# Two attention stages of a hybrid decoder: from a scheduled order to a fixed stream with two-bank steps

## The chip, the core and the metric

One core of a Trainium2 chip runs the whole program. The metric is the device time in microseconds (us). Engines: PE (matrix multiply, its weight loads listed as PEld), DVE (vector), ACT (scalar), POOL (general), SP (issues DMAs). PE writes its results into PSUM, eight banks of 128 partitions x 512 f32 columns; the other operands are in SBUF.

## What is computed

Two layers over 2048 tokens of width 1024. Layer 0 mixes tokens with multi-head latent attention (12 heads, query and key of 64 + 32 rotary), layer 1 with forgetting attention (12 heads of 64, the cumulated log forget gate added to the logits). Both have 4 heads of cross-attention to 256 memory tokens.

```python
def causal_block_attention(q, k, v, scale, log_f_cum=None):
    s = jnp.einsum('bqhd,bkhd->bhqk', q_i, k) * scale          # for each block of 128 queries
    if log_f_cum is not None:
        s = s + (f_q[..., None] - f_t[:, :, None, :])
    s = jnp.where(key_pos[None, :] <= q_pos[:, None], s, -jnp.inf)
    return jnp.einsum('bhqk,bkhd->bqhd', softmax(s), v)

h = h + rms_norm((concat(main, mem_out) * silu(gate)) @ w_out[i], norm_post[i])
```

## The kernel before

The stages follow each other: `proj_a` and `up_a` (projections of layer 0), the attention of layer 0, `out_proj(0)`, `proj_b` (layer 1), the attention of layer 1, `out_proj(1)`. To keep f32 accuracy each operand is split into a high and a low part (`hi` at L170, `lo` at L189), and a product is two or three matmul passes.

An attention stage works unit by unit. A unit (`Unit`, L1374) is one head and one group g of 512 queries; for a memory head it has 256 keys, for a causal head 512(g+1). A head has 17,408 logit columns of 128 keys each. For each unit there are these parts:

- **Maxima** (`max_closures`, L1421): a matmul at L1454 with queries on the partitions writes up to 512 keys into one bank, and DVE takes the row maximum: a plain reduce at L1461, or at L1458, for the chunk with the diagonal, a custom instruction that adds the causal mask `mqk` first and writes a junk tile, followed by a read of its accumulator. `nm` (L1466) negates, `nm_row` (L1477) transposes through PE (L1480), ACT copies the row (L1482) and issues the small DMA that puts it into the query operand (L1483). That the maximum is then part of the logits matmul is why the row must be there before the unit's logits start.
- **Steps** (`main_closures`, L1487). A wide step has 1024 logit columns, a narrow one 256. A head has 16 wide and 4 narrow steps, a memory unit one wide step. Keys are on the partitions. `s_half` (L1533) works in halves of one bank: matmuls at L1550 (three passes in layer 0, two in layer 1; L1525 and L1529 add the causal mask), ACT's exp of the half from PSUM (L1553), and after the last half ACT's copy to f16 (through L173), and the subtraction that gives the low part (L195), of which POOL does a share and DVE the rest (`POOL_SHARE`, L53: 0.45 of the columns in layer 0, 0.75 in layer 1).
- **Values** (`pv_steps`, L1562): 3 matmuls of 64 or 65 columns (L1575) for each 128x128 block of probabilities, in batches of two steps. `finish` (L1579) divides and stores; ACT issues that DMA (L1592).

`run_units` (L1202) writes the units in program order with maxima ahead of the steps by a count of microseconds (`LEAD`), loads of queries, keys and values in between, and values at a raised priority (L1277). The tile framework then schedules: it takes instructions of all engines by priority when its own model finds them ready, so the order on each engine isn't the written one. Banks: maxima 1 to 4, logits 5 to 7 one at a time, values 0. There are 4 buffers for each of `ph` and `pl` (the f16 high and low parts).

Buffers that a DMA will overwrite are first touched by POOL (`hold`, L1008, a copy of one word), so that the wait for their last reader is POOL's. SP issues nearly all loads (L970 and others), POOL those at L1341. In layer 0 POOL also splits the output weights (`w_split`, L1100: 1024 columns at L180 and L195 for each of 8 tiles). 8 memory units of layer 0 and 12 of layer 1 run early, beside the end of the projections (`att_start`, L973). `out_proj`'s matmuls are at L1173.

Of the kernel before, what the change touches and what calls it, by code (L numbers as in the profile page):

```python
# [21 lines left out]
P = 128  # L22
# [6 lines left out]
G = 512  # L29
# [23 lines left out]
POOL_SHARE = {"mla": 0.45, "fox": 0.75, "mem": 0.5}  # L53
LOGP = 8.0 * math.log(2.0)
# [84 lines left out]


# [12 lines left out]
class Banks:  # L153
# [5 lines left out]
    def tile(self, shape, dtype, name=None, tag=None):  # L159
        self.k += 1  # L160
        return view(self.mem, self.banks[(self.k - 1) % len(self.banks)] * G, shape, dtype, name)


class Trunk:
# [64 lines left out]
    def constants(self, ctx):  # L229
# [16 lines left out]
                                pattern=[[1, P]], channel_multiplier=-1)  # L246
        ones = cp.tile([P, P], F32, name="ones")
# [725 lines left out]
    def att_start(self, l):  # L973
# [5 lines left out]
        else:  # L979
# [8 lines left out]
        ap["qq"] = Turn(*(Later(lambda b=b, k=k: b.tile([P, 2, G], F32R, name=f"qq{k}")) for k, b in enumerate(qqs)))  # L988
        ap["ym"] = Turn(*(ymp.tile([P, 4, 2 * DH], F32, name=f"ym{k}") for k in range(4)))
        ap["nr"] = Turn(*(nrp.tile([4, P], F32R, name=f"nr{k}") for k in range(4)))  # L990
        ap["vrm"] = Turn(vrp.tile([P, MEMH * NMEM // P, DH], F32, name="vrm"))
        mqk = self.mqk = sp.tile([P, G], BF16, name="mqk")
        ap["mj"] = Turn(sp.tile([P, G], BF16, name="mj"))
        ap["pm"], ap["ps"], ap["pv"] = self.banks(2, 3), self.banks(5, 6), self.banks(0)
        self.l, self.yt = l, {}
        nc.gpsimd.memset(mqk, 0.0)
        nc.gpsimd.affine_select(out=mqk[:, G - P:G], in_=mqk[:, G - P:G], compare_op=ALU.is_ge, fill=NEG, base=0,
                                pattern=[[-1, P]], channel_multiplier=1)
# [7 lines left out]
        run_units([mem], first)  # L1006

    def hold(self, word):  # L1008

        self.hi("pool", word, self.ap["nr"].tiles[0][0:1, 0:1].bitcast(F32))  # L1010
# [29 lines left out]
    def attention(self):  # L1040
# [5 lines left out]
        ap["pm"], ap["ps"], ap["pv"] = self.banks(1, 2, 3, 4), self.banks(5, 6, 7), self.banks(0)  # L1046
# [53 lines left out]
        def w_split(c):  # L1100
            w = ap["vr"].next().rearrange("p (c t) d -> p c (t d)", c=2)
            self.hold(w[0:1, 0, 0:1])
            nc.sync.dma_start(out=w, in_=self.i["w_out"][l, c * P:(c + 2) * P, :].rearrange("(c p) d -> p c d", p=P))
            for k in range(2):
                tiles(c + k)
                self.hi("pool", W[c + k][0], w[:, k])
                self.lo("pool", W[c + k][1], w[:, k], W[c + k][0])

        def w_load(c):
            tiles(c)  # L1110
            for k in range(2):
                self.hold(W[c][k][0:1, 0:1])
                self.load_r(W[c][k], self.ws[c, k])
        if l == 0:
            extra = [(4 + c, 0.55, lambda c=c: w_split(c)) for c in range(0, KC, 2)]
# [86 lines left out]
def run_units(heads, objs, extra=()):  # L1202

    n = len(objs)
    maxq, late = [], []
    for u, o in enumerate(objs):
        for j, (f, c) in enumerate(o.max_closures()):
            maxq.append((u, f, c))
            if j == 1 and late:
                maxq.append(late.pop())  # L1210
        maxq.append((u, o.nm, 0.0))
        late.append((u, o.nm_row, 0.0))
    maxq.append(late.pop())
    t = acc = lead = 0.0
    need = [0.0] * n
    for u, f, c in maxq:
        need[u] += c
    span = {}
    rate = sum(need) / sum(c for o in objs for _, _, c in o.main_closures())
    for u, o in enumerate(objs):  # L1220
# [3 lines left out]
        t += sum(c for _, _, c in o.main_closures())  # L1224
        span[o.hd.idx] = (span.get(o.hd.idx, (t0, 0))[0], t)
    lead += LEAD[heads[0].l]
    aux = [(-1.0, hd.idx, f) for hd in heads[len(heads) > 1:2] for _, f in hd.prep()]
# [5 lines left out]
    for h, fr, f in extra:  # L1233
        a, b = span[h + 1]
        aux.append((a + fr * (b - a), 99, f))
    aux.sort(key=lambda x: (x[0], x[1]))
    st = dict(k=0, done=0.0, dma=0)
    pend = []
# [18 lines left out]
    def advance(main, target):  # L1257
        while st["k"] < len(maxq):
            u, f, c = maxq[st["k"]]
            if u > main and not (st["done"] <= target and u <= main + AHEAD):  # L1260
# [5 lines left out]
            f()  # L1266
            st["done"] += c
            st["k"] += 1

    def flush():  # L1270
        while pend:
            o = pend[0][0]
            ends = [x[3] for x in pend if x[0] is o][:BATCH]
            m = len(ends)
# [370 lines left out]
```

## Time and profile before

| what | value |
|---|---|
| median of 3 runs | 2985.06 us (2978.82 to 2997.47) |
| the profiled execution's own time | 2981.39 us |
| its span from first to last instruction | 2979.7 us |
| mean granted PE clock | 0.966 |
| PE, DVE, ACT, POOL busy | 95%, 59%, 44%, 37% of the span |

The attention of layer 0 lies at about 638 to 1294 us of the span, that of layer 1 at 2170 to 2800 us. Busy times are unions of the records of one engine; consecutive records of an engine can overlap, so the distance between starts is shorter than a record.

### The profile page before, as it was taken

How to read it: one execution, taken by the hardware profiler on the slowest of the kernel's cores; microseconds unless marked ns; L12 is line 12 of the kernel's file. 1: busy time of each engine (PE TensorE's matmuls, PEld its weight loads, DVE VectorE, ACT ScalarE, POOL GpSimd, SP SyncE). 2: the span in 40 equal slices, each digit the busy share in tenths (PEclk: the TensorE clock that was granted, in tenths of full speed). 3: DMA queues.
4: the chain of work that ended last, by engine and by line, in shares of the span. 5: the costliest groups of instructions: out<-in, count | busy, mean ns of one | idle time of the engine just before them, and what ended most of it. 6: DMA issues, size and time to landing. Idle time of an engine off the chain costs nothing.

```text
span 2979.7 us, 60697 instructions
## 1 busy us (share of the span) xinstructions
PE 2815.9 (95%) x24017; PEld 2389.2 (80%) x24017; DVE 1765.3 (59%) x3710; ACT 1312.8 (44%) x2315; POOL 1095.8 (37%) x1190
## 2 busy tenths in 40 slices
PE   7999999889999999999999999999889799999999
PEld 6789998657888788788889978998567677777887
DVE  6422215568898999754553364101378799999444
ACT  5321123347777777642230010111257687777421
POOL 2110124344556655642000023100135566676521
PEclk9999999879999999999999999999868899999999
DMA  5332447762343323255343139723433334353453
GB/s 188 127 132 90 126 163 259 248 191 74 80 101 85 90 80 87 80 176 203 128 137 103 59 125 311 236 76 109 129 101 93 102 102 115 103 159 118 166 178 117
DMA packets 261685, 398.23 MB, mean 134 GB/s; under 512 B 25196, under 2 KB 141436, under 8 KB 261292
## 3 DMA queue, kind: packets, MB, share of 16 engines
q1 hardware_dynamic: 146032, 237.25, 27.8%
q10 hardware_dynamic: 113832, 155.32, 14.4%
q8 instruction: 189, 3.10, 0.4%
q0 software_dynamic: 1536, 1.77, 0.3%
q14 instruction: 96, 0.79, 0.1%
HBM read 237.83 MB, written 156.17 MB: 132 GB/s over the span
## 4 chain that ended last, share of the span: by engine, by line
PE 73%; DVE 12%; DMA 8%; issue 3%; ACT 1%; POOL 1%; ACTq 0%; SPq 0%; DVEq 0%; POOLq 0%
PE banks L226 34%; PE banks L1550 12%; PE banks L1173 12%; PE banks L1575 8%; PE banks L1454 4%; DVE bA L195 4%; DVE mx L1461 4%; DVE bA L1458 1%; DMA qs<-bA 1%; PE banks L1148 1%; PE banks L306 1%; DMA qrs<-bA 1%; PE banks L1435 1%; ACT bA L173 1%; DMA bA<-qbs 1%
## 5 line engine op out<-in xcount | busy, mean ns | idle before, releaser
L195 POOL TENSOR_TENSOR bA<-bA,bA 128x768 f16<-128x768 f32 (+7 forms) x306 | 435.8, 1432 | 344.2 <-ACT bA L173 277.2
L226 PE MATMUL banks<-bR,bA 128*128 128x256 f32 (+3 forms) x4437 | 552.9, 287 | 0.6 <-DVE bQ L467 0.6
L226 PEld LDWEIGHTS banks<-bR,bA 128*128 128x128 f32 x4437 | 544.3, 190 | 5.4 <-DVE bQ L467 0.8
L226 PE MATMUL banks<-bA,bR 128*128 128x512 f32 (+2 forms) x2208 | 515.0, 389 | 6.7 <-ACT bS L780 4.2
L1553 ACT ACTIVATE bA<-banks 128x512 f32<-128x512 f32 (+1 forms) x771 | 419.9, 569 | 216.4 <-PE banks L1550 124.6
L1550 PE MATMUL banks<-bA,bA 96*128 96x512 f32 (+13 forms) x1808 | 499.8, 381 | 5.0 <-DMA bA<-bA 2.5
L226 PEld LDWEIGHTS banks<-bA,bR 128*128 128x128 f32 x2208 | 401.3, 191 | 93.5 <-ACT bS L780 4.9
L1461 DVE TENSOR_REDUCE mx<-banks 128x1 f32<-128x512 f32 x576 | 377.3, 679 | 39.3 <-PE banks L1454 37.4
L1550 PEld LDWEIGHTS banks<-bA,bA 96*128 96x128 f32 (+3 forms) x1808 | 324.7, 195 | 46.8 <-DMA bA<-bA 3.1
L173 ACT ACTIVATE bA<-bA 128x1024 f16<-128x1024 f32 (+5 forms) x335 | 280.9, 853 | 143.6 <-PE banks L1575 34.0
L1454 PE MATMUL banks<-bA,bA 73*128 73x512 f32 (+5 forms) x864 | 292.0, 398 | 23.4 <-DVE mx L1458 14.0
L195 DVE TENSOR_TENSOR bA<-bA,bA 128x256 f16<-128x256 f32 (+4 forms) x267 | 250.5, 942 | 89.8 <-ACT bA L173 89.6
L195 DVE TENSOR_TENSOR bR<-bR,bR 128x1024 fp32r<-128x1024 f32 (+6 forms) x134 | 136.1, 1018 | 189.2 <-POOL bR L180 169.4
L195 POOL TENSOR_TENSOR bR<-bA,bR 128x512 f16<-128x512 f32 (+2 forms) x167 | 183.7, 1102 | 165.6 <-ACT bR L173 87.6
L1575 PEld LDWEIGHTS <-bA 128*128 128x128 f16 x5280 | 183.8, 101 | 55.1 <-issue 27.3
L1173 PE MATMUL banks<-bA,bA 128*128 128x512 f32 x960 | 227.4, 391 | 0.0
L1454 PEld LDWEIGHTS banks<-bA,bA 73*128 73x128 f32 (+1 forms) x864 | 163.2, 199 | 69.3 <-DVE mx L1458 23.6
L1550 PE MATMUL banks<-bR,bA 128*128 128x512 f32 (+6 forms) x624 | 212.6, 405 | 3.2 <-ACT bA L1553 1.9
L1575 PEld LDWEIGHTS <-bR 128*128 128x128 f16 x5280 | 174.2, 99 | 45.1 <-issue 15.9
L180 POOL TENSOR_SCALAR bR<-bR 128x1024 fp32r<-128x1024 f32 (+3 forms) x50 | 60.5, 1212 | 406.8 <-PE banks L226 367.5
L1173 PEld LDWEIGHTS banks<-bA,bA 128*128 128x128 f32 x960 | 178.5, 188 | 36.1
L1575 PE MATMUL banks<-bA,bR 128*128 128x65 f16 (+1 forms) x4896 | 175.2, 195 | 9.3 <-DVE bR L195 7.9
(218 smaller groups left out, 3607.1 us busy)
## 6 DMA issues: line engine op xcount, KB each, us to landing
bA<-qbs SPq DMA_DIRECT2D x65, 256.0 KB
bA<-in_x_dram SPq DMA_DIRECT2D x32, 512.0 KB
gs<-bG ACTq DMA_DIRECT2D x128, 128.0 KB
bA<-gs SPq DMA_DIRECT2D x32, 512.0 KB
bA<-ys SPq DMA_DIRECT2D x32, 512.0 KB
bA<-h SPq DMA_DIRECT2D x28, 512.0 KB
ks<-bA ACTq DMA_DIRECT2D x24, 512.0 KB
qs<-bA ACTq DMA_DIRECT2D x24, 512.0 KB
```

The source lines that it names most:

```text
L173: nc.scalar.activation(out, in_, AF.Copy, scale=scale)
L180: nc.gpsimd.tensor_scalar(out, in_, scale, 0.0, op0=ALU.mult, op1=ALU.add)
L195: e.tensor_tensor(out=out, in0=in_, in1=hi, op=ALU.subtract)
L226: nc.tensor.matmul(out, lhsT=a, rhs=b, start=start and i == 0, stop=stop and i == n - 1)
L306: nc.tensor.transpose(pt[:, j, :], out[:, c * P:(c + 1) * P], self.idf)
L1148: nc.tensor.transpose(pt[:, j, :], gt[:, c * P:(c + 1) * P], self.idf)
L1173: nc.tensor.matmul(ps[:, ns], lhsT=a, rhs=b[:, ns], start=c == 0 and j == 0, stop=c == KC - 1 and j == 2)
L1454: nc.tensor.matmul(ps[:, 0:w], lhsT=q[0:qr, t * P:(t + 1) * P], rhs=k[0:kr, c * G:c * G + w], start=True, stop=True)
L1461: nc.vector.tensor_reduce(out=self.mx[:, t, c:c + 1], in_=ps[:, 0:w], axis=AX.X, op=ALU.max)
L1550: nc.tensor.matmul(ps[:, o:o + bw], lhsT=k[0:kr, (self.k0 + kt) * P:(self.k0 + kt + 1) * P], rhs=q[0:qr, q0:q0 + bw], start=i == 0 and not ...
L1553: nc.scalar.activation(pf[:, half:half + hw], ps[:, 0:hw], AF.Exp, scale=self.scale)
L1575: nc.tensor.matmul(self.pv[:, t, 0:n], lhsT=p[:, o:o + P], rhs=v[:, kv, a:a + n], start=self.first, stop=False, skip_group_check=True)
```

## The change

Both attentions are emitted inside `manual_schedule` for PE, ACT, DVE, POOL and SP: each engine gets these instructions in the order in which they are written.

- A step is one piece (`flow`): logits of both halves in two neighbouring banks of a ring of four (banks 4 to 7), one exp of up to 1024 columns, one f16 copy, and for wide steps one POOL subtraction of all 1024 columns. DVE subtracts for narrow steps only, one step later (`flow_lo`).
- Maxima have banks 1 to 3. The causal mask is added by a matmul of 128 columns, and the plain reduce writes the negated maximum. The constant that `nm` added is now the bias of the exp. The row's copy is DVE's and its DMA SP's; so is the DMA of the result.
- There are 6 `ph` and 6 `pl` buffers (5 at the end of layer 1); values are written 3 steps behind the logits, half of a step's maxima ahead of its logits and half behind.
- All `hold`s are gone, and the load at L1341 goes to SP. In layer 0 the output weights are loaded before their split, and split in 32 pieces of 256 columns, the high part by ACT.
- Early memory units are written by `run_early`, one unit of maxima ahead, still scheduled by the framework.

```diff
+    def flow(self, blocks, box):
+        K, nc, ap = self.K, self.K.nc, self.K.ap
+        w = box["w"] = max(b[1] + b[3] for b in blocks)
+        ps = ap["ps"].tile([P, 2 * G], F32, name="ps", tag="ps")
+        pf, ph, pl = (ap[x].next() for x in ("pf", "ph", "pl"))
+        box.update(pf=pf, ph=ph, pl=pl)
+        for half in range(0, w, G):
+            self.s_bank(blocks, half, box, ps[:, half:half + G])
+            self.s_logits(blocks, half, box[half])
+        nc.scalar.activation(pf[:, 0:w], ps[:, 0:w], AF.Exp, scale=self.scale, bias=LOGP)
+        K.hi("act", ph[:, 0:w], pf[:, 0:w])
+        if w > G:
+            K.lo("pool", pl[:, 0:w], pf[:, 0:w], ph[:, 0:w])
+    def flow_lo(self, box):
+        w = box["w"]
+        if w <= G:
+            self.K.lo("dve", box["pl"][:, 0:w], box["pf"][:, 0:w], box["ph"][:, 0:w])
...
-        ap["pm"], ap["ps"], ap["pv"] = self.banks(1, 2, 3, 4), self.banks(5, 6, 7), self.banks(0)
+        ap["pm"], ap["ps"], ap["pv"] = self.banks(1, 2, 3), BankRing(self.psum, 4, 4), self.banks(0)
...
-        run_units(heads, units, extra)
+        order = {getattr(mybir.EngineType, x) for x in ("PE", "Activation", "DVE", "Pool", "SP")}
+        with self.tc.manual_schedule(engines=order):
+            run_units(heads, units, extra, fewer)
...
+    for i, (u, s, w) in enumerate(steps):
+        o = objs[u]
+        run_aux(t)
+        lag[0] = len(K.ap["ph"].tiles) - 3
+        todo = advance(u, min(t * rate + lead, RUNUP * (t + 4 * G) + need[0]))
+        while todo and not o.has_row:
+            todo.pop(0)()
+        m = len(todo) // 2
+        for f in todo[:m]:
+            f()
+        before, box = box, {}
+        o.flow(s, box)
+        for f in todo[m:]:
+            f()
+        close()
+        if before:
+            before[0].flow_lo(before[1])
...
+        values(i)
...
-                    if diag:
-                        junk = ap["mj"].next()
-                        nc.vector.tensor_tensor_reduce(out=junk[:, 0:w], in0=ps[:, 0:w], in1=K.mqk[:, G - w:G], scale=1.0, scalar=-3.0e38,
-                                                       op0=ALU.add, op1=ALU.max, accum_out=self.mx[:, t, c:c + 1])
+                    if diag:
+                        nc.tensor.matmul(ps[:, w - P:w], lhsT=K.idb, rhs=K.mqk, start=True, stop=False, skip_group_check=True)
...
-        nc.scalar.activation(nr, ps, AF.Copy)
-        nc.scalar.dma_start(out=self.nmrow.bitcast(F32), in_=nr.bitcast(F32))
+        nc.vector.tensor_copy(nr, ps)
+        nc.sync.dma_start(out=self.nmrow.bitcast(F32), in_=nr.bitcast(F32))
...
-            if h > 1:
-                K.hold(kt[0:1, 0, c][:, 0:1])
...
+        def w_split(c, k, n):
+            w, (h, lo) = wr[c][:, k, n:n + 2 * P], (x[:, n:n + 2 * P] for x in W[c + k])
+            self.hi("act", h, w)
+            self.lo("pool", lo, w, h)
```

## Rows read from the trace of the kernel before

**Rows 1.** Busy time of each engine in five stretches (first row: the columns).

```profile
core 0: us, PE busy (x) PEld busy (x) DVE busy (x) ACT busy (x) POOL busy (x), PEclk, DMA share, GB/s
560.00:638.00 78.00, 61.44 (x315) 46.21 (x315) 46.19 (x85) 28.22 (x50) 33.55 (x35) 0.81 0.79 245
638.00:1294.00 656.00, 631.25 (x7451) 523.30 (x7452) 565.08 (x1200) 470.81 (x765) 358.23 (x417) 0.97 0.34 91
800.00:900.00 100.00, 99.93 (x1232) 83.21 (x1231) 94.98 (x209) 79.29 (x129) 50.97 (x66) 1.00 0.35 88
...
2075.00:2170.00 95.00, 76.46 (x440) 56.94 (x438) 33.94 (x64) 23.44 (x40) 15.79 (x21) 0.90 0.45 132
2170.00:2800.00 630.00, 572.42 (x6916) 451.44 (x6917) 530.27 (x1125) 452.59 (x759) 405.94 (x405) 0.93 0.40 114
```

**Rows 2.** The same view of the out projection's matmuls (L1173) alone, both attention stretches.

```profile
638.00:1294.00 656.00, 12.60 (x50) 8.98 (x51) 0.97 0.34 91
2170.00:2800.00 630.00, 15.86 (x63) 11.59 (x64) 0.93 0.40 114
```

**Rows 3.** Chain that ended last, shares by line: first layer 0's attention, then layer 1's.

```profile
by line: PE banks L1550 41.9%; PE banks L1575 21.1%; PE banks L1454 13.6%; issue 3.6%; DMA bA<-qrs 2.3%; DVE bR L195 2.0%; DMA bA<-in_w_out_dram 1.8%; PE banks L1173 1.7%; DVE mx L1461 1.6%; PE banks L1435 1.0%; PE banks L1525 0.9%; DMA bA<
...
by line: DVE bA L195 16.5%; DVE mx L1461 15.0%; PE banks L1575 13.5%; PE banks L1550 13.3%; issue 7.6%; DVE bA L1458 6.6%; PE banks L1454 5.8%; DMA bA<-qbs 3.3%; DVE nm L1474 2.9%; PE banks L1173 2.3%; DVE bR L1588 1.8%; DMA bA<-kbs 1.8%; A
```

**Rows 4.** Pieces of that chain in layer 0, 860 to 880 us: start, us, what.

```profile
865.82 1.45 PE banks L1550 x6
867.28 1.47 PE banks L1575 x48
...
872.12 0.07 PE banks L1525
```

**Rows 5.** Pieces of that chain that wait for DMAs, both attentions: start, us, what.

```profile
640.59 5.77 DMA bA<-qrs
...
1005.34 5.39 DMA bA<-in_w_out_dram
...
1100.03 6.40 DMA bA<-in_w_out_dram
...
2163.59 6.44 DMA bA<-qbs
...
2263.53 11.04 DMA bA<-kbs
...
2318.11 14.28 DMA bA<-qbs
```

**Rows 6.** Groups of instructions by shape in layer 1's attention: xcount | busy us, mean ns.

```profile
L195 POOL TENSOR_TENSOR bA<-bA,bA 128x768 f16<-128x768 f32 x192 | 323.2, 1686 | 138.7 <-ACT bA L173 93.6 <-issue 15.7 <-PE banks L1550 12.5
L1553 ACT ACTIVATE bA<-banks 128x512 f32<-128x512 f32 x402 | 225.2, 592 | 91.4 <-PE banks L1550 49.9 <-DVE r L1583 15.3 <-DVE bA L195 6.8
L173 ACT ACTIVATE bA<-bA 128x1024 f16<-128x1024 f32 x201 | 211.3, 1055 | 46.2 <-PE banks L1575 34.0 <-DVE bR L1588 3.6 <-DMA bA<-kbs 2.8
L195 DVE TENSOR_TENSOR bA<-bA,bA 128x256 f16<-128x256 f32 x192 | 189.3, 986 | 30.7 <-ACT bA L173 30.6
...
L1553 ACT ACTIVATE bA<-banks 128x256 f32<-128x256 f32 x48 | 17.9, 374 | 5.1 <-PE banks L1575 2.7 <-PE banks L1550 1.3 <-DVE bA L195 1.1
```

**Rows 7.** Timeline of layer 1's attention near 2407 us: start, us, engine, line, operation.

```profile
2406.48 5.16 SPq L970 DMA_DIRECT2D bA<-kbs  x4
...
2406.95 1.65 POOL L195 TENSOR_TENSOR bA<-bA,bA 128x768 f16<-128x768 f32 x1 [1.17 <-ACT bA L173]
...
2407.01 1.88 DVE L195 TENSOR_TENSOR bA<-bA,bA 128x256 f16<-128x256 f32 x1
...
2411.20 0.41 DVE L195 TENSOR_TENSOR bA<-bA,bA 128x256 f16<-128x256 f32 x1
```

**Rows 8.** POOL's subtraction of 512 columns in the timeline of layer 0.

```profile
849.49 1.16 POOL L195 TENSOR_TENSOR bR<-bA,bR 128x512 f16<-128x512 f32 x1 [1.70 <-issue]
```

**Rows 9.** POOL's subtraction of 1024 columns with an f32 result, groups of layer 0's attention.

```profile
L195 POOL TENSOR_TENSOR bA<-bA,bA 128x1024 fp32r<-128x1024 f32 x6 | 14.9, 2485 | 0.0
```

More of the change, by code (lines that the diff above doesn't have):

```diff
@@ L138, in next, with keep @@
         return self.tiles[(self.k - 1) % len(self.tiles)]
+    def keep(self, n):
+        m = len(self.tiles)
+        order = [(self.k + j) % m for j in range(m)]
+        self.tiles = [self.tiles[j] for j in order if j < n]
+        self.k = 0
 class Later:
@@ L1005, in att_start @@
             u.q = ap["qq"].next()
[L1006 to L1010 removed]
+        run_early(mem, first)
     def k_ones(self, j):
@@ L1199, in out_proj, with run_early, rows, ends @@
                 yield
-def run_units(heads, objs, extra=()):
+def run_early(mem, objs):
+    K = mem.K
+    for _, f in mem.prep():
+        f()
+    pend = []
+    def rows(u):
+        for f, _ in u.max_closures():
+            f()
+        u.nm_row()
+    def ends(m):
+        while len(pend) > m:
+            o, s, box, _ = pend.pop(0)
+            with K.tc.high_priority(offset=PV_AHEAD):
+                o.pv_steps([(s, box)])
+            o.finish()
+    for u in objs[:2]:
+        u.q_dma()
+    rows(objs[0])
+    for k, u in enumerate(objs):
+        if k + 2 < len(objs):
+            objs[k + 2].q_dma()
+        if k + 1 < len(objs):
+            rows(objs[k + 1])
+        for pre, f, _ in u.main_closures():
+            pre()
+            f(pend)
+        ends(1)
+    ends(0)
+def run_units(heads, objs, extra=(), fewer=None):
+    K = heads[0].K
     n = len(objs)
@@ L1223, in run_units @@
         t0 = t
-        t += sum(c for _, _, c in o.main_closures())
+        t += width[u]
         span[o.hd.idx] = (span.get(o.hd.idx, (t0, 0))[0], t)
-    lead += LEAD[heads[0].l]
-    aux = [(-1.0, hd.idx, f) for hd in heads[len(heads) > 1:2] for _, f in hd.prep()]
+    lead += ROW_AFTER + 3 * 2 * G
+    aux = [(-1.0, hd.idx, f) for hd in heads[1:2] for _, f in hd.prep()]
     for hd in heads[2:]:
@@ L1424, in max_closures, with start, reduce @@
         out = []
+        def start():
+            self.nmv = K.sm.tile([P, 4], F32R, name="nm", tag="nm", bufs=AHEAD + 2)
+        def reduce(to, ps, negate):
+            nc.vector.tensor_reduce(out=to, in_=ps, axis=AX.X, op=ALU.max, negate=negate)
         if not self.causal:
@@ L1464, in max_closures @@
+                    nc.tensor.matmul(ps, lhsT=q[0:qr, t * P:(t + 1) * P], rhs=k[0:kr, x:x + w],
+                                     start=not diag, stop=True, skip_group_check=diag)
+                    if self.nchunk == 1:
+                        reduce(self.nmv[:, t:t + 1], ps, True)
+                    else:
+                        reduce(self.mx[:, t, c:c + 1], ps, False)
+                out.append((f, min(G, nk - c * G)))
         return out
     def nm(self):
-        K, nc = self.K, self.K.nc
```

199 lines of the change are left out of this document (113 added, 86 removed).

## The prediction

> **What bounds the kernel now.** I read first the busy time by stage, then the chain that ended last, then the groups and the timeline inside the attentions. Outside the attentions nothing changes; inside, the two layers differ.
>
> In layer 0 PE is busy for 631 of 656 us and DVE for 565 [rows 1], and the chain lies on PE's logits, values and maxima for 77% (L1550, L1575, L1454); DVE's two largest lines have 3.6% [rows 3]. The reader should see that PE is the limit there and DVE, 86% busy, is not. In layer 1 PE is busy for 572 of 630 us, but the chain has moved: DVE's subtraction (L195), maxima (L1461, L1458), `nm` and final scaling take 16.5 + 15.0 + 6.6 + 2.9 + 1.8 = 42.8%, against 32.6% for the same three PE lines [rows 3]. DVE ends most waits there.
>
> A busy PE is no PE at its peak, so I measure what PE needs by a stretch in which it never stands: 800 to 900 us, busy 99.93 us, 1232 matmuls [rows 1]. Layer 0's attention has 7451 matmuls, 50 of them the out projection's [rows 1, 2]: 7401 / 12.32 = 601 us, and 13 us for those 50, together 614. So 656 - 614 = 42 us are not PE work. Layer 1 has no such stretch, so I take layer 0's 601 us and correct it. It has one logits pass less: 12 heads x 34 blocks of 512 columns at 1.45 / 6 = 0.242 us [rows 4] = 99 us. It has 4 memory units less in the stage; each is 4 logits blocks (0.97), 1024 columns of maxima (0.48) and 24 value matmuls at 1.47 / 48 = 0.031 us (0.73) [rows 4]: 9 us in all. 601 - 99 - 9 = 493, with the out projection's 16 us [rows 2] 509, and 630 - 509 = 121 us are not PE work. The change can win at most these 42 + 121 = 163 us, and something in the early stretches.
>
> **The change part by part.** *DVE.* In layer 1 the 192 subtractions of 256 columns go, 189 us of DVE's 530 [rows 1, 6]. Their mean is 0.99 us, but one that runs alone takes 0.41 us, and the one of 1.88 us at 2407.01 began while POOL's record at 2406.95 ran and outlasted it by 0.29 [rows 7]: two thirds of a long one is waiting for POOL. DVE keeps 48 narrow subtractions (12 heads x 4), each between 0.41 us and 0.41 plus a whole POOL operation (2.14, below), 20 to 122 us. The row copies that it takes over are some 52 of about a quarter microsecond (nearest row: ACT's exp of 256 columns, 0.37 [rows 6], a bound from above; from below nothing), at most 19 us. So DVE falls from 530 to between 361 and 482 us, below PE's 509. The custom maxima lose their accumulator reads; I count nothing for that, since DVE is then under PE.
>
> *POOL.* 512 columns take 1.16 us [rows 8], 768 take 1.65 [rows 7]: 0.49 for 256 more, so 1024 take 2.14 us; from above, 2.49 with an f32 result [rows 9]. I take 2.14, as the f16 result is the case here. Layer 1 has 196 wide steps in the stage (12 x 16 and 4 memory units): 419 us, at most 488. Layer 0 has 200: 428 us, plus the value and weight splits, which are no more than what POOL does there beside L195 today. Both stay below PE.
>
> *ACT.* 256 more columns of exp cost 0.592 - 0.374 = 0.218 us, so one exp of 1024 costs 0.592 + 2 x 0.218 = 1.03 instead of 2 x 0.592 = 1.18 [rows 6]. A wide step is 1.03 + 1.06 = 2.09 us, 196 of them 410; the narrow steps, 0.37 + about 0.4 each, add 37: 447 us against PE's 509. The 32 weight pieces of layer 0 (each near 0.4) are 13 us on ACT, beside PE work.
>
> *PE.* 192 more mask matmuls in each layer. In the chain one costs 0.07 us [rows 4]: 13 us a layer, 26 together, on the path because PE now sets it. Bounds: 0 (it hides behind another weight load) and 0.14, twice the row.
>
> *Order and waits.* Logits of step i wait for the exp of step i-2 (two pairs of banks); values of a pair are written at least 3 steps after its second step. From logits to the low part it is 1.03 + 1.06 + 2.14 = 4.2 us; in three steps PE does, in layer 1, 3 x (4 x 0.242 + 2 x 0.242 + 24 x 0.031) = 6.6 us of logits, maxima and values. So 2.4 us of slack covers one late POOL operation. What is queued on PE behind a late pair is the next step's maxima and logits, so ACT would starve one step later. Steps are uneven and POOL is over 80% full in layer 1, so I don't count this as free.
>
> *What stays.* The chain of layer 1 holds three waits for loads of queries and keys in its first 160 us, 6.4 + 11.0 + 14.3 = 32 us; layer 0 has 5.8 us at its start [rows 5]. Loads stay on SP in much the same number, so I leave 30 us in layer 1. In layer 0 the wait for output weights (5.4 us in the row shown, 6.4 in a second) should go, since they are loaded before POOL meets the split; with one late query load in mid-stage I leave 10 us there.
>
> *Neutral.* The early memory units are rewritten too. PE isn't busy for 16.6 and 18.5 us there [rows 1]; I count 0, with half of that, 17 us, as the bound each way. The out projection starts inside both attentions, 12.6 + 15.9 = 28.5 us of PE time [rows 2]. If nothing can be put between the ordered instructions, this comes back as tail, at most 28.5 us; I count 0, because the order binds only what is written inside it.
>
> *The sum.* Layer 0: 42 - 13 - 10 = 19 us won. Layer 1: 121 - 13 - 30 = 78 us. Together 97. The profiled execution took 2981.4 us, 3.7 us under the median of the runs shown, its span 2979.7: 2981.4 - 97 = 2884 us.
>
> **The rivals.** *A clean stream.* No stall is left at all: 163 - 26 = 137 us, 2844 us. For it: between 800 and 900 us PE already does this. Against it: the load waits of [rows 5] have a cause that the change keeps.
>
> *Little of it arrives.* The overlap with the out projection is lost (28.5) and layer 1 keeps another 30 us of pipeline waits, since four engines are then between 65 and 95% full with two logits buffers: 2884 + 58 = 2942 us. For it: POOL and ACT are both above 400 us per layer.
>
> *The narrow subtraction blocks DVE.* It waits for half a POOL operation, 1.07 us, 48 times a layer, maxima queue behind it in order, three banks fill, and PE stands: 96 x 1.07 = 103 us, 2987 us, no change. For it: the 1.88 us row [rows 7]. Against it: DVE would have 27 us or more to spare in layer 1, and maxima run several steps ahead. The Trainium skill (SBUF — State Buffer, section Who interferes with whom) calls the pair of ports that DVE and GpSimd share an exclusive lock, held for the whole instruction, and counts a DVE instruction with two SBUF inputs among those that contend, but no reduce; the row of 1.88 us beside POOL's 1.65 agrees, and by that rule longer POOL operations mean longer waits for each DVE subtraction that is left.
>
> *Slower: SP becomes the queue that all wait for.* The small row DMAs and the stores now stand behind the big loads, and without `hold` a load waits on SP itself for PE's last read. Four key loads kept SP for 5.16 us [rows 7]; a head of layer 1 has eight, 10.3 us. If at each of 22 head changes the rows came that much too late, it would cost 22 x 10.3 = 227 us: 3111 us. It decides against the change from 97 / 22 = 4.4 us per head on. Against it: maxima, and so rows, lead by about 11,500 columns, some 11 steps.
>
> **How the numbers follow.** Forecast 0.51, clean stream 0.18, little arrives 0.14, blocked DVE 0.10, SP 0.07. The time is that of the forecast, 2884 us. The range reaches down past the clean stream with a gain in the early stretches (2844 - 17, and some for PE's masks hidden), 2815, and up to "little arrives", 2945. One per cent, 30 us, is about what a measurement of this kernel can tell from no change. Faster by more: the first three cases, 0.83; within 1%: 0.09; slower: 0.08.
>
> **What would show it.** In layer 1's attention DVE's busy time falls under 480 us and its share of the chain under 15%; PE's lines take over 70% of the chain. POOL's group of 1024 columns shows about 2.14 us, ACT's exp of 1024 about 1.03. The stage of layer 1 shrinks four times as much as that of layer 0. The forecast is wrong if layer 0 shrinks by over 45 us (then my PE time there contains stalls), if POOL's subtraction takes 2.5 us or more, if waits of L1550 for the row DMA or of L1575 for POOL add up to over 40 us, or if PE's granted clock in layer 1 stays near the 0.93 of [rows 1].

## The result: 5.8% slower, and the profile after

The changed kernel takes 3158.1 us (3146.6 to 3166.1, 4 runs), the kernel before 2981.9 us beside it: ratio 1.058, 95% interval 1.0524 to 1.0637. The profiled execution took 3146.6 us, its span is 3144.8, 165 us over the span before. From the first maximum to the last value matmul, layer 0's attention grew by 105 us and layer 1's by 53; the part behind layer 1's attention grew by 14, that between the two shrank by 8. The stages in the view of busy time (columns as in [rows 1]), after:

```profile
638.00:1403.00 765.00, 669.03 (x7577) 537.21 (x7577) 424.16 (x804) 464.44 (x536) 477.34 (x280) 0.91 0.29 74
2263.00:2950.00 687.00, 583.56 (x7120) 457.44 (x7119) 382.43 (x778) 452.54 (x512) 437.93 (x219) 0.89 0.40 110
```

Layer 0 took 656 us and takes 765, layer 1 took 630 and takes 687 [rows 1]. DVE fell as forecast (530 to 382 us in layer 1, within the 361 to 482 worked out), POOL's and ACT's loads are close to the forecast, and yet PE stands for 96 and 103 us where it stood for 25 and 58. No other engine is busy for more than 66% of either stage, so no engine's total of work is the limit; the chain shows what PE waits for.

The terms that were sizes came out right. Groups by shape in layer 1's attention, after (xcount | busy us, mean ns):

```profile
L219 POOL TENSOR_TENSOR bA<-bA,bA 128x1024 f16<-128x1024 f32 x158 | 336.0, 2141 | 159.2 <-issue 66.0 <-ACT bA L197 35.1 <-PE banks L1560 16.2
...
L1628 ACT ACTIVATE bA<-banks 128x1024 f32<-128x1024 f32 x196 | 199.4, 1017 | 183.0 <-PE banks L1686 176.1 <-POOL bA L219 3.1 <-PE banks L1559 2.0
...
L219 DVE TENSOR_TENSOR bA<-bA,bA 128x256 f16<-128x256 f32 x45 | 29.5, 655 | 14.5 <-ACT bA L197 14.5
```

POOL's whole step is 2.14 us (worked out: 2.14), ACT's exp of 1024 columns 1.02 (1.03). Then the chain that ended last, layer 0's attention first, layer 1's second, to be held against [rows 3]. (L1686, L1702, L1560 are the logits, values and maxima, L1550, L1575 and L1454 before; L221 is DVE's low part of the values in layer 0.)

```profile
by line: PE banks L1686 38.3%; PE banks L1702 20.6%; PE banks L1560 14.8%; DVE bA L221 4.5%; DVE mx L1526 3.5%; issue 2.2%; DVE bR L219 2.0%; PE banks L1559 2.0%; ACT bA L1628 1.5%; ACT bR L197 1.2%; DVE bA L1715 1.1%; DMA bA<-bR 0.9%; PE b
...
by line: PE banks L1686 24.4%; PE banks L1702 21.8%; DMA bA<-bA 17.1%; PE banks L1560 12.8%; DVE mx L1526 4.2%; issue 2.6%; ACT bA L1628 2.1%; DVE bR L1715 1.7%; POOL bA L219 1.6%; DMA bA<-qms 1.5%; PE banks L1559 1.4%; DMA bR<-bA 1.2%; ACT
```

Of DVE's 42.8% in layer 1 little is left. In their place stands `DMA bA<-bA`, the row of maxima on its way into the query operand: 17.1% of 687 us, 117 us. Before it had 1.5%, 9 us, behind the end of the line shown in [rows 3].

**Layer 1.** The waits there, and below them pieces of the chain around one of them (start, us, what):

```profile
PE banks L1686 <- DMA bA<-bA: 65.1, 12, 12.5
```

```profile
2492.60 0.88 PE banks L1686 x4
2493.48 12.32 DMA bA<-bA
2505.85 1.65 PE banks L1686 x3
2507.50 0.43 PE banks L1560
2507.92 2.65 PE banks L1702 x48
```

There are 12 such waits, about one a head. SP's timeline shows that SP did not hold this row back: DVE's copy ran from 2493.18 to 2493.45, the DMA was issued at 2493.48, and landed 12.3 us later.

```profile
2488.38 1.18 SPq L998 DMA_DIRECT2D bA<-qbs  x2
...
2490.10 0.52 SPq L998 DMA_DIRECT2D bA<-qbs  x1
2490.67 0.62 SPq L998 DMA_DIRECT2D bR<-qbs  x1
2493.48 1.28 SPq L1579 DMA_DIRECT2D bA<-bA  x1
```

What was in the queue ahead of it is seen in the DMA view of 2486 to 2506 us (40 slices of half a microsecond; tenths busy of 16 DMA engines, and what they moved):

```profile
DMA  0099596379967995111113931111296331111111
GB/s 0 0 296 285 183 203 98 111 188 287 295 163 169 309 240 115 57 49 55 49 53 130 357 123 50 49 37 47 82 229 127 107 111 37 53 49 49 52 42 48
```

The burst of a head's loads fills slices 3 to 16. Then come stretches of "1": about two engines of 16 busy, near 50 GB/s, while another load in between reaches 357. 256 KB at 50 GB/s is 5 us. The second query load of each unit does that, the one that fills both halves of a tile with one pattern (`bR<-qbs` at 2490.67, and one of the two `bA<-qbs` at 2488.38); run g1_qa2 below shows it. The row stands behind these two in the same queue; before the change it had ACT's queue.

**Layer 0.** No such row wait; there PE's masks of maxima (L1559) wait for a bank. Timeline of DVE, then POOL, then PE, after:

```profile
1012.06 0.69 DVE L1526 TENSOR_REDUCE mx<-banks 128x1 f32<-128x512 f32 x1 [0.94 <-PE banks L1560]
1016.70 4.18 DVE L221 SCALAR_TENSOR_TENSOR bA<-bA,vsc 128x256 f16<-128x256 f32 x4 [3.94 <-POOL bA L204]
1020.80 0.68 DVE L1526 TENSOR_REDUCE mx<-banks 128x1 f32<-128x512 f32 x1
...
1014.08 2.13 POOL L219 TENSOR_TENSOR bR<-bR,bR 128x1024 f16<-128x1024 f32 x1 [1.35 <-ACT bR L197]
1016.18 2.17 POOL L204 TENSOR_SCALAR bA<-bA,vsc 128x256 f16<-128x256 f32 x4
...
1013.86 0.36 PE L1560 MATMUL banks<-bA,bR 96*128 96x256 f32 x1
1021.53 0.27 PE L1559 MATMUL banks<-mqk,idb 128*128 128x128 bf16 x1 [7.31 <-DVE mx L1526]
```

Read it from DVE. It has four value splits (L221) next in its order. They need POOL's high parts (L204), which POOL has behind a whole step, which waits for ACT. So DVE stands 3.94 us and then works 4.18 us on the splits, while finished maxima wait in banks 1 to 3 for the reduces behind them. PE fills the three banks and stands for 7.31 us, with its next matmuls in the queue behind. 8 such waits at L1559 add up to 51.5 us.

**The clock.** In the stalls and behind them the granted clock is lower (view of busy time, after; the clock is the last column but two; the first row lies behind the stall in layer 0, the second for the most part in that of layer 1):

```profile
1022.00:1029.00 7.00, 7.00 (x54) 5.55 (x54) 3.52 (x9) 2.04 (x2) 0.00 (x0) 0.70 0.00 0
...
2501.00:2508.00 7.00, 2.15 (x9) 1.44 (x10) 0.04 (x1) 0.41 (x1) 0.00 (x0) 0.50 0.20 63
```

0.50 is the lower of PE's two levels, 1.2 GHz. In the 7 us behind five of the row waits (from 2506, 2609, 2712, 2822 and 2874 us on) it was 0.50 to 0.69. The 48 value matmuls after the row's wait take 2.65 us where [rows 4] has 1.47, and where the same chain has 1.61 at 2486.14 us, ahead of the wait. So a stall costs more than its length: in layer 0 PE stands 71 us longer than before and is also busy 38 us longer, 13 of which the prediction had counted for the masks.

### The profile page after: what moved, and what is told of

Its sections match the earlier page's. It is cut to its first block, busy times and chain, and to the rows that moved or that the text cites. A ratio compares the mean times of both kernels' runs of the same rounds, so it can differ in the third digit from the quotient of the medians.

```text
span 3144.8 us, 59145 instructions
## 1 busy us (share of the span) xinstructions
PE 2883.4 (92%) x24401; PEld 2425.8 (77%) x24401; DVE 1473.2 (47%) x2954; ACT 1303.8 (41%) x1823; POOL 1260.0 (40%) x869
## 3 DMA queue, kind: packets, MB, share of 16 engines
q1 hardware_dynamic: 181064, 255.18, 28.5%
## 4 chain that ended last, share of the span: by engine, by line
PE 80%; DMA 8%; DVE 7%; ACT 2%; issue 2%; POOL 1%; ACTq 0%; SPq 0%; DVEq 0%; POOLq 0%
PE banks L250 33%; PE banks L1686 15%; PE banks L1206 11%; PE banks L1702 10%; PE banks L1560 6%; DMA bA<-bA 4%; DVE mx L1526 2%; DVE bA L221 1%; PE banks L1181 1%; ACT bA L1628 1%; PE banks L1559 1%; PE banks L334 1%; ACT bA L197 1%; DVE bR L219 1%; DMA bA<-bR 1%
## 5 line engine op out<-in xcount | busy, mean ns | idle before, releaser
L1526 DVE TENSOR_REDUCE mx<-banks 128x1 f32<-128x512 f32 (+2 forms) x864 | 519.3, 620 | 464.6 <-PE banks L1560 461.1
L219 POOL TENSOR_TENSOR bA<-bA,bA 128x1024 f16<-128x1024 f32 (+5 forms) x277 | 502.6, 1826 | 387.5 <-ACT bA L197 198.9
L1686 PE MATMUL banks<-bA,bA 96*128 96x512 f32 (+13 forms) x1808 | 502.4, 390 | 70.1 <-DMA bA<-bA 64.1
L1628 ACT ACTIVATE bA<-banks 128x1024 f32<-128x1024 f32 (+1 forms) x409 | 364.9, 892 | 373.1 <-PE banks L1686 341.9
L1686 PEld LDWEIGHTS banks<-bA,bA 96*128 96x128 f32 (+3 forms) x1808 | 340.2, 202 | 121.0 <-DMA bA<-bA 68.9
L197 ACT ACTIVATE bA<-bA 128x1024 f16<-128x1024 f32 (+5 forms) x400 | 335.2, 846 | 84.5 <-DMA qrs<-bA 13.8
L1560 PE MATMUL banks<-bA,bA 73*128 73x512 f32 (+5 forms) x864 | 338.6, 434 | 1.6 <-DMA bA<-qbs 0.9
L1702 PEld LDWEIGHTS <-bA 128*128 128x128 f16 x5918 | 211.4, 102 | 53.0 <-issue 32.5
L1206 PE MATMUL banks<-bA,bA 128*128 128x512 f32 x960 | 226.9, 392 | 0.0
L204 POOL TENSOR_SCALAR bR<-bR 128x1024 fp32r<-128x1024 f32 (+3 forms) x50 | 61.4, 1229 | 409.0 <-PE banks L250 379.1
L1686 PE MATMUL banks<-bR,bA 128*128 128x512 f32 (+6 forms) x624 | 208.1, 401 | 9.2 <-DMA bR<-bA 9.2
L1560 PEld LDWEIGHTS banks<-bA,bA 73*128 73x128 f32 (+1 forms) x864 | 170.2, 206 | 53.6 <-issue 38.5
L219 POOL TENSOR_TENSOR bR<-bR,bR 128x1024 f16<-128x1024 f32 (+2 forms) x75 | 161.4, 2152 | 116.4 <-ACT bR L197 63.1
L1206 PEld LDWEIGHTS banks<-bA,bA 128*128 128x128 f32 x960 | 179.3, 189 | 36.3
L219 POOL TENSOR_TENSOR bR<-bA,bR 128x1024 f16<-128x1024 f32 (+2 forms) x74 | 148.7, 2013 | 104.8 <-ACT bR L197 50.9
L1177 POOL TENSOR_TENSOR bA<-bA 128x512 f32<-128x512 f32 x64 | 99.5, 1577 | 212.7 <-DMA bA<-gs 202.5
L493 ACT ACTIVATE bG<-banks 128x256 f32<-128x256 f32 x128 | 49.1, 385 | 288.3 <-PE banks L250 224.6
L219 DVE TENSOR_TENSOR bR<-bR,bR 128x1024 fp32r<-128x1024 f32 (+5 forms) x66 | 74.0, 1125 | 184.6 <-POOL bR L204 170.2
```

The source lines that it names most:

```text
L197: nc.scalar.activation(out, in_, AF.Copy, scale=scale)
L204: nc.gpsimd.tensor_scalar(out, in_, scale, 0.0, op0=ALU.mult, op1=ALU.add)
L219: e.tensor_tensor(out=out, in0=in_, in1=hi, op=ALU.subtract)
L493: nc.scalar.activation(st[:, 0:2 * P], ps[:, 0:2 * P], AF.Silu)
L1177: nc.gpsimd.tensor_tensor(out=gt[:, hs], in0=gt[:, hs], in1=yt[:, hs], op=ALU.mult)
L1206: nc.tensor.matmul(ps[:, ns], lhsT=a, rhs=b[:, ns], start=c == 0 and j == 0, stop=c == KC - 1 and j == 2)
```

## The experiments

My theory A: layer 0 is lost to DVE's fixed order, layer 1 to rows that land late. The main rival B: a fixed order as such; remove one late thing and the next takes its place. L0 and L1 below are the profiled execution's stretches from the first maximum to the last value matmul, in us. They come from one execution each, between 12.5 us under its run's median (g4; the changed kernel 11.5 under) and 19 us over it (e5). The kernel before, run beside each group, had medians of 2973.6 to 2981.9 us, so a difference between medians of two groups can be off by some 8 us: g1's 82 us below are 72 by the ratios.

| run | median | ratio to before, interval | L0 | L1 |
|---|---|---|---|---|
| before / after | 2981.9 / 3158.1 | 1.058 (1.0524 to 1.0637) | 655 / 760 | 629 / 682 |
| e1_row_act | 3123.8 | 1.0481 (1.0454 to 1.0508) | 775 | 645 |
| e2_v_late | 3082.3 | 1.0341 (1.0316 to 1.0367) | 692 | 682 |
| e3_both | 3038.4 | 1.0197 (1.017 to 1.0224) | 687 | 645 |
| e4_free | 3018.1 | 1.0124 (1.0094 to 1.0154) | 662 | 636 |
| e5_row_y_act | 3135.0 | 1.0535 (1.0513 to 1.0557) | 776 | 662 |
| e7_row_y_v | 3126.0 | 1.0508 (1.0492 to 1.0524) | 751 | 667 |
| e8_sp_free | 3137.7 | 1.0547 (1.0502 to 1.0592) | 778 | 642 |
| e9_free_row_y | 2998.2 | 1.0078 (1.0062 to 1.0093) | 660 | 611 |
| f1_before_pool | 2978.2 | 0.9996 (0.9978 to 1.0015) | 652 | 621 |
| f2_v_late | 3085.8 | 1.0368 (1.034 to 1.0397) | 690 | 686 |
| f3_pe_only | 3034.0 | 1.0195 (1.0166 to 1.0224) | 661 | 645 |
| f4_dve_free | 3062.5 | 1.0284 (1.0256 to 1.0312) | 671 | 681 |
| g1_qa2 | 3075.7 | 1.0338 (1.0313 to 1.0363) | 761 | 596 |
| g2_before_qa2 | 2937.5 | 0.9878 (0.9852 to 0.9904) | 659 | 605 |
| g3_free_qa2 | 2938.3 | 0.9889 (0.9866 to 0.9911) | 657 | 577 |
| g4_fixed_all | 2998.4 | 1.0081 (1.005 to 1.0112) | 679 | 599 |
| h2_pool_qa2 | 2937.5 | 0.9858 (0.983 to 0.9886) | 653 | 604 |
| h1_best | 2915.7 | 0.9798 (0.9775 to 0.9821) | 652 | 577 |

**The first four: one cause each, both, and no order.**

```diff
# e1_row_act
-        nc.sync.dma_start(out=self.nmrow.bitcast(F32), in_=nr.bitcast(F32))
+        nc.scalar.dma_start(out=self.nmrow.bitcast(F32), in_=nr.bitcast(F32))
# e2_v_late (and: v_hi and v_lo are no longer forced by the next head's maxima)
-                for at, f in ((0.02 + 0.05 * k, v_dma), (0.34 + 0.06 * k, v_hi), (0.35 + 0.06 * k, v_lo)):
+                for at, f in ((0.02 + 0.05 * k, v_dma), (0.34 + 0.06 * k, v_hi), (0.46 + 0.06 * k, v_lo)):
# e4_free
-        with self.tc.manual_schedule(engines=order):
+        if True:
```

e1_row_act:

> The changed kernel (3158 us) with one edit: the DMA of the row of maxima is issued by ACT instead of SP, so it goes in a queue of its own and no longer behind the loads; the copy stays on DVE. Theory A (what is lost in layer 1 is the row DMA landing some 12 us after its issue, behind loads of 1.3 MB in the same queue, once per head): the chain's 117 us of waits for the row DMA in layer 1 go, about 12 us for each of 12 heads less a few that something else ends next: 100 to 130 us won, 3030 to 3060 us, and layer 0 stays at 765 us. Rival B (the fixed order itself is the loss: whatever comes late stops every engine, and the next late thing takes the place): under 40 us won, over 3118 us. Rival C (DVE's late reduces are what makes the row late): no gain, 3150 us or more.

e2_v_late:

> The changed kernel with one edit, in layer 0 alone: DVE's low part of the values is written two steps behind POOL's high part instead of right behind it, and neither is forced early by the first maxima of the next head. Theory A (in layer 0 DVE stands for the value split with the reduces queued behind it, three banks fill, PE stands 7 us and its clock falls, once per head): 12 heads x 6 to 9 us = 70 to 110 us won, 3050 to 3090 us, all in layer 0, whose attention shrinks from 765 to about 670 us. Rival B (fixed order: the next late thing takes its place): under 30 us won, over 3128 us. Rival D (POOL's whole-step subtractions in layer 0 are what is late, for the probabilities too): no gain, 3150 us or more.

e3_both:

> Both edits: row DMA issued by ACT, and the low part of the values two steps behind the high part. Theory A: the gains add, as they lie in different layers: 3158 - 115 - 90 = 2953 us (2930 to 2990), at or a little under the kernel before (2982). Rival B: over 3090 us. If each alone wins little but both win much, one cause hid behind the other.

e4_free:

> The changed kernel with the order of the instructions no longer held fixed in the two attentions (the same stream is written, but the scheduler may move instructions as in the kernel before); banks, buffers, masks, whole-step subtractions and the queue of the rows stay as changed. Theory A (the rows lie behind the loads in the queue of SP, and the value split is badly placed): layer 1 keeps its 12 us per head, as the queue stays, layer 0 may win its 70 to 100 us, and some 20 us of overlap with the output projection come back: 3030 to 3080 us. Rival B (the fixed order is the loss): under 2990 us. Rival D (the new banks, masks and POOL's whole steps are the loss): 3130 us or more.

In e2 and e3 some values are read after the output weights have overwritten them; f2 below takes that away and has the same time. Layer 0 did what theory A said (-76 us). Layer 1 did not: rows on ACT won 34 us, rival B's number. e3 won 120 us, far from theory A's 2953 us. The chain of e1 shows why: the rows wait less, and now the queries wait.

```profile
2560.79 11.54 DMA bR<-qbs
...
2572.39 4.97 DMA bA<-bA
```

A query load issued last in a burst of SP's landed 11.5 us later, and the maxima and the row followed it. Without a fixed order (e4) 140 us came back, 98 of them in layer 0, a little more than theory A's range and less than rival B's; of the 65 us that PE's logits waited for rows in layer 1, 48.5 stayed.

**The second four: SP's order, and POOL's part earlier.** e5 also sends the stores of y from ACT (the same edit at L1719). e7 adds to it `(0.24 + 0.04 * k, v_hi), (0.34 + 0.04 * k, v_lo)`. e8 takes SP out of the names in `order`. e9 is e4 with rows and stores from ACT.

> The changed kernel with the row DMAs and the stores of y issued by ACT, as in the kernel before; the order stays fixed, SP is left with loads alone. With the rows alone on ACT it took 3124 us, and there SP stood about 150 us in layer 1 for DVE's final scaling of y, with the loads of queries and keys behind it in order, and a query load then landed 11.5 us after its issue once per two heads. Theory A2 (in a fixed order SP's small DMAs that wait for results hold up the loads behind them, and the loads then come in a burst): those waits go, 50 to 90 us more than 3124, 3035 to 3075 us, nearly all in layer 1. Rival B (the fixed order makes any late thing stop all): ACT now stands for DVE's final scaling with the exps behind it, under 25 us won, over 3100 us.

> As the kernel with rows and stores on ACT, and in layer 0 POOL's high part of the values is written some two steps earlier in the stream (0.24 + 0.04 k of a head instead of 0.34 + 0.06 k, DVE's low part at 0.34 + 0.04 k), so that DVE finds it done. Theory A: layer 0's attention shrinks by 60 to 80 us against the kernel with rows and stores on ACT alone, 2965 to 3010 us in all. Rival B: under 30 us. Rival E (POOL, moved earlier, stands for the last reading of the value buffer by the head before, its subtractions behind it): no gain, the stall moves to POOL.

> The changed kernel with SP left out of the fixed order: the scheduler may place the loads, rows and stores, all still issued by SP; PE, ACT, DVE and POOL keep their order. Theory A2 (SP's order is the loss in layer 1): the loads get round the waiting rows and stores, layer 1 wins 60 to 110 us, 3050 to 3100 us in all, and layer 0 stays at about 765 us. Rival F (the queue, not the order of issue: rows and loads share one queue, and a row lands only after the loads before it): under 30 us won, over 3128 us. Rival B (the order of the other four engines): the same, over 3128 us.

> The changed kernel with no fixed order at all (3018 us by itself) and rows and stores issued by ACT, as before the change: of the change it keeps two-bank steps, six buffers, POOL's whole-step subtractions, the masks for the maxima and their own banks. Theory A2: in the run without fixed order PE's logits in layer 1 still waited 45 + 52 us for the row DMA; those go, 70 to 110 us won, 2910 to 2950 us, faster than the kernel before (2979). Rival F (the rest of the stream is slower by itself): under 30 us won, over 2988 us, not faster than before.

In all four the theory that forecast the gain (A2, in e7 A) missed. e5 won nothing over e1 (+11 us), e8 only 20 us: SP's waits in order are long in the list of waits but hold little of the time. (In e8's profiled execution layer 1 is 40 us shorter and layer 0 18 us longer.) So I had the wrong part of theory A in layer 1, and the number that came in e8 was that of rival F, the queue itself. e7 moved POOL's half out of DVE's way and won 9 us over e5, for the burst on DVE stayed:

```profile
1004.44 0.91 DVE L221 SCALAR_TENSOR_TENSOR bA<-bA,vsc 128x256 f16<-128x256 f32 x1
1005.73 2.96 DVE L221 SCALAR_TENSOR_TENSOR bA<-bA,vsc 128x256 f16<-128x256 f32 x2 [0.38 <-POOL bA L204]
1009.07 2.33 DVE L221 SCALAR_TENSOR_TENSOR bA<-bA,vsc 128x256 f16<-128x256 f32 x1 [0.38 <-POOL bA L204]
1011.32 0.68 DVE L1526 TENSOR_REDUCE mx<-banks 128x1 f32<-128x512 f32 x1
...
1012.06 0.26 PE L1559 MATMUL banks<-mqk,idb 128*128 128x128 bf16 x1 [6.06 <-DVE mx L1526]
```

(Timeline of e7, DVE and PE.) The four splits still stand together with no reduce between them, since the first maxima of the next head force what is left of its preparation into one step. DVE is taken for 6.9 us, PE stands 6.06.

**The third four: the counted-on term alone, and whose order costs.** f1 is the kernel before with `"fox": 1.0` in place of 0.75 in `POOL_SHARE`. f2 is e2 with loading and splitting of the output weights moved to 0.72 of a head and after. f3 holds PE alone in order, f4 all but DVE.

> The kernel before with one part of the change alone: in layer 1 POOL subtracts whole steps (share 1.0 instead of 0.75), DVE's 192 subtractions of 256 columns are gone there. The prediction counted on this for most of layer 1's gain. Theory G (it was right about this term): DVE's busy time in layer 1 falls by about 180 us, its subtraction (16.5% of the chain there, 104 us) leaves the chain, and 25 to 70 us are won, 2910 to 2955 us. Rival H (POOL's 2.14 us for each step end as late as DVE's did): within 15 us of 2979 us.

> The changed kernel with the low part of the values in layer 0 two steps behind the high part and not forced early, as in the earlier run (3082 us), and with the loading and splitting of the output weights moved from 0.5 to 0.72 of a head and after, so that the values are no longer overwritten before they are read. Theory A (DVE's four splits in a burst, with the reduces queued behind them, are layer 0's loss): 3070 to 3100 us, layer 0's attention near 695 us instead of 765. Rival I (in the earlier run it was the weights, whose loads the splits then waited for, that moved something): over 3120 us.

> The changed kernel with only PE held in the written order; the scheduler may move the instructions of ACT, DVE, POOL and SP. With no order held it took 3018 us, with all five held 3158 us, with SP alone free 3138 us. Theory A (in order, it is DVE's splits in layer 0 and SP's loads in layer 1 that stand in others' way): most of the 140 us come back, 3020 to 3060 us. Rival J (PE's own order is the loss: PE stands at the head of its queue for a bank or a row with other work ready behind it): over 3110 us.

> The changed kernel with DVE alone left out of the fixed order. Theory A: DVE's reduces get in front of the value splits in layer 0, 50 to 80 us won there and nothing in layer 1: 3080 to 3110 us. Rival J (PE's order): under 20 us won, over 3138 us.

f2 and f4 settle layer 0: splits spread out between reduces win 70 us there, DVE free 89, and DVE free wins nothing in layer 1. f3 has layer 0 at 661 us, as with no order at all: PE's own order costs 16 us in all (3034 against 3018). So rival J, PE's order, falls, and in layer 0 most of the loss was the order on DVE. The order on ACT and on POOL was not tried by itself.

f1 is the surprise. Stage of layer 1 (view of busy time, 2166 to 2790 us), then its chain (2160 to 2790 us: shares, and two pieces of one kind):

```profile
2166.00:2790.00 624.00, 562.87 (x6927) 457.29 (x6928) 379.57 (x917) 454.27 (x764) 486.42 (x405) 0.92 0.40 115
```

```profile
by line: PE banks L1550 23.7%; PE banks L1575 19.4%; PE banks L1454 12.7%; POOL bA L195 6.2%; DMA bA<-frd 5.8%; DMA bA<-qbs 4.3%; issue 3.5%; DVE nm L1474 3.3%; DMA bA<-kbs 2.7%; PE banks L1173 2.7%; DVE mx L1461 1.9%; SPq L970 1.6%; DVE bA
...
2366.92 6.13 DMA bA<-frd
...
2499.21 6.03 DMA bA<-frd
```

DVE lost 150 us of busy time and most of its share of the chain, PE's three lines rose from 32.6% to 55.8%, and the ratio is 0.9996: theory G's relief came and its gain did not. POOL (6.2%) and loads took the place: the decay rows (`frd`), which POOL issues and which now stand behind its longer subtractions, and the queries.

**The last six: the slow load.** One edit, in g1 to the changed kernel, in g2 to the kernel before:

```diff
-            K.load_r(qa, src[:, 0].unsqueeze(0).to_broadcast([2, DH, G]))
+            for d in (0, DH):
+                K.load_r(qa[d:d + DH], src[:, 0])
```

g3 is e9 with it; g4 is the changed kernel with it, rows on ACT and f2's splits. h2 is g2 with f1's share, h1 is h2 with the load of `frd` issued by SP.

> The changed kernel (3158 us), fixed order, rows on SP; only the query load of layer 1 that fills two halves of a tile through one pattern with a leading 2 is written as two loads of 64 partitions. Theory K (that load moves on about 2 of 16 DMA engines, some 5 us, and rows wait behind two of them): the row's 12 us per head fall to 3 or less, 70 to 120 us won, 3040 to 3090 us, layer 0 as it was. Rival L (rows and loads are late because SP issues them late, in order): under 25 us won, over 3133 us.

> The kernel before with the same edit alone: the query load written as two loads of 64 partitions. Theory K: its chain in layer 1 held 3.3% (21 us) for query loads and 1.8% for key loads that share the queue: 10 to 40 us won, 2940 to 2970 us. Rival M (with the rows in a queue of their own, query loads are early enough): within 8 us of 2981 us.

> The changed kernel with no order held, rows and stores on ACT (2998 us), and the query load written as two. Theory K: layer 1 wins another 10 to 40 us: 2958 to 2988 us, near the kernel before. Rival M: within 8 us of 2998 us.

> The changed kernel in fixed order with three edits: rows issued by ACT, DVE's low part of the values two steps behind the high part (weights moved behind them), and the query load written as two. Singly the first two won 34 and 72 us. Theory K: all three together win 34 + 72 + 50 to 100 us, 2950 to 3000 us, so that order and queue were nearly all that the changed kernel lost. Rival B (a fixed order always has a next late thing): over 3030 us, no better than the sum of the first two.

> The kernel before with two edits: the query load written as two (2937 us by itself), and POOL subtracting whole steps in layer 1. Theory N (the loads of frd that POOL issues stand behind its longer subtractions and take back what DVE gives up): within 10 us of 2937 us. Rival O (the query loads alone took the gain back): 25 us or more won, under 2912 us.

> The same with the load of frd issued by SP instead of POOL, as in the changed kernel. Theory N: with both successors gone the shift to POOL is worth 20 to 45 us: 2890 to 2917 us. Rival P (POOL, near 500 us of busy time, ends as late as DVE did, whatever the loads do): within 10 us of 2937 us.

g1 wins 82 us with rows still on SP, all of it in layer 1 (682 to 596). The wait for rows in its list:

```profile
PE banks L1687 <- DMA bA<-bA: 4.2, 4, 1.8
```

65.1 us became 4.2 (L1687 is the line of the logits there). The Trainium skill (DMA: Bandwidth & Descriptors, section Rules for kernel authors) says that an outermost dimension of c below 16, such as a leading broadcast of c copies, keeps the whole DMA on at most c engines; the stretches of "1" at 50 GB/s above agree for c = 2. With two plain loads they are gone from the same view (g1, 2455 to 2475 us, again half a microsecond a slice):

```profile
DMA  7889787997568200000000000100000114949689
GB/s 217 201 234 221 107 221 172 224 296 172 107 176 242 90 12 0 0 0 0 0 0 0 0 0 0 33 0 0 0 0 4 82 66 123 172 102 180 181 265 308
```

The same stretches are in the trace of the kernel before (2480 to 2490 us, a quarter of a microsecond a slice):

```profile
DMA  1111136996689975211111111111111111999311
```

g4, inside theory K's range, adds up to most of the loss: 160 us of the 176, where the three edits won 34, 72 and 82 singly. g3 won 60 us over e9, more than theory K's 10 to 40, and so stands where g2 does, at 2938 us. That answers a question that the earlier runs leave open: with the query load mended in both and no order held, the rest of the change is worth nothing in sum. In the profiled executions layer 1 is 28 us shorter in g3 than in g2 (577 against 605), but 21 us are lost between the attentions and behind the second, and 9 ahead of the first. Layer 1 of g3 in the view of busy time:

```profile
2172.40:2749.60 577.20, 560.22 (x7106) 439.39 (x7107) 415.19 (x769) 442.39 (x510) 435.42 (x215) 0.95 0.46 122
```

h2 and h1 answer f1: with the queries fast and `frd` still on POOL the shift to POOL is worth nothing clear of noise (2937.5 both; ratios 0.988 and 0.986), with `frd` on SP 22 us. (The move of `frd` without the shift was not run; in g2 no wait for `frd` is in the list.) Layer 1 of h1, with the start of the out projection (2160 to 2740 us):

```profile
by line: PE banks L1551 30.2%; PE banks L1576 23.9%; PE banks L1455 16.4%; DVE nm L1475 4.8%; PE banks L1173 4.0%; DMA bA<-frd 3.1%; DVE mx L1462 3.1%; issue 2.2%; DVE bA L1459 1.6%; POOL bA L195 1.3%; ACT bA L173 1.2%; ACT bA L1554 1.1%; P
```

PE's three lines have 70.5%. h1 is 2.0% faster than the kernel before and the fastest of all; beside the split query load, which is no part of the change, it has of the change only POOL's whole steps in layer 1 and the queue of `frd`.

## Why the prediction was wrong

The forecast was 2884 us, and "slower" had 0.08. Two of its own signs of being wrong came: PE's logits waited 65 us for rows in layer 1, where 40 was the limit, and the granted clock there was 0.89, under the 0.93 of [rows 1].

- **The first step that failed: "Loads stay on SP in much the same number, so I leave 30 us in layer 1."** I counted loads and not the small DMAs that moved in behind them. Waits for rows alone came to 117 us of the chain. The rival that SP becomes the queue all wait for (0.07, 10.3 us a head) had the place and nearly the price of one wait: the chain has ten pieces of 6.4 to 16.9 us, over its decision point of 4.4, but in layer 1 only. That its total, 3111 us, lies near the measured 3158 is luck, since layer 0 has the larger part of the loss for another reason. Its mechanism was off: not the time that SP needs to issue, but two-engine query loads ahead in the queue (e8: SP's order 20 us; g1: the loads 82 us). These loads were there to be seen in the trace of the kernel before (its DMA view above). I argued against it that maxima lead by some 11 steps; the lead is in the writing, but a query load that lands late makes maxima and row late with it.
- **The second: "In layer 0 ... I leave 10 us there."** I took POOL's value splits as busy time and never asked what stands behind DVE's half of them in a fixed order. "Order and waits" followed one late POOL operation into the probabilities, where 2.4 us of slack did cover it; the one that hurt was late for DVE, with the reduces queued behind it and three banks to fill. It cost 70 us (f2) to 89 us (f4).
- **The third: layer 1's 121 us that "are not PE work" were taken as DVE's to give back.** The size of DVE's relief was right (382 us), its worth was not: f1 shows that by itself it is nothing, since loads end at about the same time as DVE did. The query load was in [rows 5] and I priced it as what stays, not as what is next. The 121 us were also too many. In g3 (its row above) PE stands for only 17 us of layer 1's 577 and is busy for 560, where the sum had 509 + 13 = 522. I had taken the rate of matmuls from a stretch at a granted clock of 1.00; at 0.95, some 28 of the 38 us (an estimate: 0.05 x 560) come from the clock.
- **"Neutral": the out projection's 28.5 us.** I counted 0; its first matmul (L1206) now comes at 1403.3 and 2947.7 us, with or after the last values. With no fixed order the overlap hardly comes back: in e4, e9 and g3 none of layer 0's out projection matmuls starts ahead of the last values (48 before), and 4 to 29 of layer 1's (59 before). So the reason that I weighed, that nothing can be put between ordered instructions, is not enough, and the cause stays open. It costs up to the 21 us by which g3 is longer than g2 between the attentions and behind them.
- **Right:** the sizes of POOL's, ACT's and DVE's work. "The narrow subtraction blocks DVE" was right as a mechanism with a wrong bound (below), but its chain share, 2.0% in layer 0's line above, is not the loss.

Open: with rows on ACT (e1, e5) and with SP free (e8) layer 0 is some 15 to 18 us longer in the profiled executions. PE doesn't stand longer there (94 us in the changed kernel, 95 to 96 in the three); it is busy for 680 to 682 us instead of 667, at a granted clock of 0.89 instead of 0.91. Whether the edits did that isn't shown, as the changed kernel's profiled execution had the least of its four times, 11.5 us under the median. Also open is why g4, without the three causes, is still 60 us behind g3 (46 between the profiled executions, 22 of them in each attention); g3 holds no order and has the stores on ACT.

## What to carry to other kernels

When an order becomes fixed, go through each engine and each DMA queue and ask what stands behind every instruction that can be late; totals of busy time can't show it. When work is taken off the engine that ends most waits, price the next in line from the same rows before counting a gain: here loads stood so close behind that 150 us of DVE's time were worth nothing until two of them were mended. And look in the DMA view for stretches in which one or two engines of 16 move 50 GB/s.

## What the runs showed of the hardware

A DVE subtraction of 256 columns, 0.41 us alone [rows 7], took 4.85 us, nearly twice the bound that I had given it (0.41 plus one POOL operation, 2.55). It happened to 4 of the 96 in the two attentions, all in layer 0. Timeline, after, DVE and POOL:

```profile
994.37 4.85 DVE L219 TENSOR_TENSOR bR<-bA,bR 128x256 f16<-128x256 f32 x1
...
993.31 1.43 POOL L219 TENSOR_TENSOR bA<-bA,bA 128x256 fp32r<-128x256 f32 x2
994.71 2.14 POOL L219 TENSOR_TENSOR bR<-bR,bR 128x1024 f16<-128x1024 f32 x1
996.82 2.12 POOL L219 TENSOR_TENSOR bR<-bA,bR 128x1024 f16<-128x1024 f32 x1
```

POOL's operations follow each other without a gap until 998.94, and DVE's ends 0.28 us after that. It did not get in between them, in none of the four: what it can lose is a whole run of POOL's back-to-back operations, not one of them. It isn't always so: a subtraction at 2927.46 us also met POOL operations without a gap (L219, then L1177) and took 1.69 us, to 0.28 us after the end of the first. The Trainium skill (SBUF — State Buffer, section Who interferes with whom) calls the ports that the two engines share an exclusive lock and says that the order of issue decides who blocks; the four do not agree with that, since two POOL operations that began after DVE's went ahead of it.
